# Block products of seven in chunks 1, 3, 4 and 5 of three feed-forward nets, and their sums kept in PSUM

## The chip, the cores and the metric

One core of a Trainium2 chip runs the whole program once. The metric is the device time of one execution in microseconds; the kernel before is given by the median of three runs. The profile is of one further execution of the same program.

## The reference

Two layers; each has a feed-forward net, a mixer, a cross attention and a second feed-forward net, with a layer norm after each. Sequence 256, width 1024, all in f32. Only the nets matter here:

```python
D_MODEL, SEQ, DEPTH, D_FF = 1024, 256, 2, 2816

def swiglu(x, w_gate, w_up, w_down):
    return (jax.nn.silu(x @ w_gate) * (x @ w_up)) @ w_down

for l in range(DEPTH):
    h = layer_norm(ALPHA * h + 0.5 * swiglu(h, ffn1_gate[l], ffn1_up[l], ffn1_down[l]), ...)   # nets 1 and 3
    ...
    h = layer_norm(ALPHA * h + 0.5 * swiglu(h, ffn2_gate[l], ffn2_up[l], ffn2_down[l]), ...)   # nets 2 and 4
```

The nets are called 1 to 4 in the order in which they run. Net 1 has inputs of its own to set up and takes other branches (`early is not None`).

## The kernel before

**Products.** Every f32 operand is split in two: a rounded high part (`split`, L75, a cast on ACT, `whi`) and the rest (L76, a subtraction on DVE, `wlo`). A product is three matmuls, high by high, high by low, low by high (`mm_rows`, L156 to L159, which calls L132). A weight piece is 128x1024 f32, 512 KB; it is loaded into a `raw` tile and split once, one ACT cast and one DVE subtraction for each.

**A net** (`ffn`) works through D_FF in six chunks: five of 512 columns (0 to 4) and one of 256 (5). A chunk multiplies x by its gate and up columns, and `silu(gate) * up` (`sg`) is transposed: `turn` sends `sg` through four DMAs (`dealt`, L525), two DVE transposes (L531), and one split into `ah` (ACT, L75) and `al` (DVE, L76). The product with the down weights (`both`, 24 matmuls into the `dn` banks for one pair of down pieces) needs `ah` and `al`.

A chunk of 512 is computed in one of two ways:

- `hidden` (chunk 0: `first`): 8 weight pieces, 96 matmuls of 512 columns, two DVE products of gate and up (L514).
- `by_seven`: x (2 token tiles by 2 halves of the depth) times (gate, up by the same halves) is a product of 2x2 blocks; the Winograd form needs seven block products in place of eight, 84 matmuls. It has 14 weight pieces to split and 4 sums of weight blocks on DVE (L702). The gate and up blocks are w00, w10, w01, w11. Three more block sums are made by DMAs that add into SBUF (`more`, L738, issued by POOL). Sums and differences of x come from `blocks_of_x` (`quarters`, L653 and L661, split into kTh and kTl).

Chunk 5 by seven is the same at 256 columns (84 matmuls of 256), with three block sums more made by DVE and fewer pieces (7 of 128x1024).

**Which chunk goes which way:** `sevens`, L821. In nets 2 to 4: 2, 4 and 5; in net 1: 2 and 4. The products with the down weights are handed out by `todo`: every by_seven chunk of 512 does two `both`s between its block products (`between[0]` after the third, `between[1]` after the fourth), and `later` says how many come after a chunk of the other kind.

**Sums in by_seven:** a block product is summed in PSUM (`o[0]` runs on through all of them); what is needed of it on the way is copied to SBUF (`taken`, L734, ACT) and added or subtracted there by DVE (`put`, L721, four times a chunk).

**Homes:** w00's two pieces lie in `homes[0]`. For the net's first by_seven chunk these are the tiles `spare0` and `spare1`, which hold `quarters` before.

**The order** of each engine's queue is fixed when the program is built, by a scheduler, and every engine and the DMA queue of SP work strictly in their order. `issue_after` and `manual_schedule` tie single places by hand.

Of the kernel before, what the change touches and what calls it, by code (L numbers as in the profile page):

```python
# [11 lines left out]
AF = mybir.ActivationFunctionType  # L12
ALU = mybir.AluOpType
# [47 lines left out]
def model(ctx: ExitStack, tc: tile.TileContext, t: dict, out: bass.AP):  # L61
    nc = tc.nc
# [11 lines left out]
    def split(hi, lo, src):  # L74
        rounded = nc.scalar.copy(hi, src)  # L75
        lows.append(nc.vector.tensor_tensor(lo, src, hi.bitcast(F32), op=ALU.subtract))  # L76
        return rounded
# [398 lines left out]
    def ffn(l, name, n, pend=None, last=False, early=None, started=None, following=None):  # L476
        gate, up, down = (t[f"{name}_{x}"][l] for x in ("gate", "up", "down"))
        with tc.tile_pool(name="ffn", bufs=2, reuse_waits="tile") as fp:
            acts = []
# [23 lines left out]
            def ordered(v):  # L503
                return v.rearrange("p (a k j) -> p a k j", a=4, j=32)

            def in_order(o):
                return o.rearrange("p (a j k) -> p a k j", a=4, j=32)

            def activate(s, i, og):
                return nc.scalar.activation(ordered(s[:, i, :]), in_order(og), AF.Silu)  # L510
# [154 lines left out]
            def by_seven(c0, ncol, bx, between):  # L665
                deep = 1024 // ncol

                def rows_by_columns(r):
                    return r.rearrange("p (k c) -> p k c", c=ncol)

                def pieces(*tags):
                    return [
                        rows_by_columns(
                            (fp if "spare" in g else wp).tile([P, DM], F32, tag=g, name="raw", bufs=6 if g == "raw" else 1)
                        )
                        for g in tags
                    ]

                def part_of(m, j, i):
                    k = 4 * j + deep * i  # L680
                    return m[k * P : (k + deep) * P, c0 : c0 + ncol].rearrange("(k p) c -> p k c", p=P)

                def block(m, j, to):
                    for i, x in enumerate(to):
                        loads.append(nc.sync.dma_start(x, part_of(m, j, i)))
                    return to

                if ncol == CHUNK:
                    homes = [("spare0", "spare1"), ("lng", "lnb"), ("raw", "raw")]
                    n = sevens.index(c0 // CHUNK)  # L690
                    homes = [homes[(n + i) % 3] for i in range(3)] + [("spare2", "raw")]
                else:
                    homes = [("spare2",), ("raw",), ("raw",), ("raw",)]
                w00 = block(gate, 0, pieces(*homes[0]))
                w01 = block(up, 0, pieces(*homes[1]))
                w10 = block(gate, 1, pieces(*homes[3]))

                def parts_of(r, plus=None):
                    hi, lo = [], []
                    for i in range(len(r)):  # L700
                        if plus is not None:
                            nc.vector.tensor_tensor(r[i], r[i], plus[i], op=ALU.add)  # L702
                        h = wp.tile([P, 1024], F32R, tag="whi", name="whi", bufs=8)
                        w = wp.tile([P, 1024], F32R, tag="wlo", name="wlo", bufs=8)
                        h, w = (rows_by_columns(x) for x in (h, w))
                        split(h, w, r[i])
                        hi.append(h)
                        lo.append(w)
                    return Weights(hi, lo, deep, [])

                def part_of_x(i, j):
                    d = slice(4 * j, 4 * j + 4)
                    return xTh[:, d, tok(i)], xTl[:, d, tok(i)]

                def run(o, x, w, more=False):
                    for k in range(4):
                        wh, wl = w.at(k, slice(0, ncol))
                        mm_rows(o, x[0][:, k, :], x[1][:, k, :], wh, wl, k == 0 and not more, k == 3, more)

                def put(o, a, op, b):  # L720
                    nc.vector.tensor_tensor(ordered(o), in_order(a), ordered(b), op=op)  # L721

                if ncol == CHUNK:
                    s, ef = activations(), fp.tile([P, NT, CHUNK], F32, tag="up", name="halves", bufs=1)
                else:
                    both = fp.tile([P, DM], F32, tag="spare0", name="both", bufs=1)
                    s, ef = both.rearrange("p (a i c) -> a p i c", a=2, i=NT)
                e, f = ef[:, 0, :], ef[:, 1, :]

                def bank():  # L730
                    return acc((P, CHUNK))[:, 0:ncol]

                def taken(o, bank):
                    return nc.scalar.copy(ordered(o), in_order(bank))  # L734

                def more(to, m, j):
                    for i, x in enumerate(to):
                        nc.gpsimd.dma_start(x, part_of(m, j, i), accum_op=ALU.add)  # L738

                o = [bank() for _ in range(3)]  # L740
                run(o[0], part_of_x(0, 0), parts_of(w00))
                taken(s[:, 0, :], o[0])
                run(o[1], bx[0], parts_of(w00, w01))
                more(w01, up, 1)
                run(o[2], part_of_x(0, 1), parts_of(w10))
                between[0]()
                put(s[:, 0, :], o[2], ALU.add, s[:, 0, :])
                w11 = block(up, 1, pieces(*homes[2]))
                run(o[0], bx[1], parts_of(w00, w11), True)
                if ncol == CHUNK:  # L750
                    more(w00, gate, 1)
                copied = taken(e, o[0])
                between[1]()
                nc.scalar.activation(s[:, 0, :], s[:, 0, :], AF.Silu)
                put(e, o[1], ALU.subtract, e)
                if ncol == CHUNK:
                    run(o[0], bx[2], parts_of(w01), True)
                    taken(f, o[0])
                    o.append(bank())
                    run(o[3], bx[3], parts_of(w11))  # L760
                    put(f, o[1], ALU.subtract, f)
                    run(o[0], part_of_x(1, 1), parts_of(w00), True)
                else:
                    o.append(bank())
                    run(o[3], bx[3], parts_of(w11))
                    run(o[0], bx[2], parts_of(w01), True)
                    taken(f, o[0])
                    put(f, o[1], ALU.subtract, f)
                    with tc.issue_after(copied.ins):
                        w = parts_of(w00, w10)  # L770
                    between[2]()
                    run(o[0], part_of_x(1, 1), w, True)

                def left():
                    act = activate(s, 1, o[0])
                    put(e, o[3], ALU.add, e)

                    def gate_all():
                        passed.append((act, nc.vector.tensor_tensor(s, s, ef, op=ALU.mult)))
                        return turn(s)  # L780

                    return gate_all

                return left
# [33 lines left out]
                return w, ah[:, 2 * u : 2 * u + 2, :], al[:, 2 * u : 2 * u + 2, :]  # L818


            sevens = (2, 4) if early is not None else (2, 4, 5)  # L821
            passed, dealts, turn_memory = [], [], None
            bx = []

# [20 lines left out]
                            rows_of(a, i, k, m, c == u == k == 0, apart)  # L845

            todo = [(c, u) for c in range(4) for u in range(2)]
            later = (0, 0, 0, 2, 0, 2) if early is None else (0, 1, 0, 1, 0, 2)
            for c, (c0, ncol) in enumerate(chunks):
                if not c:  # L850
                    acts.append(first()())
# [11 lines left out]
                    )  # L863
                else:
                    acts.append(hidden(c0)() if ncol == CHUNK else last_hidden(c0, turn_memory))
                if c == 1 and early is None:
                    bx.extend(blocks_of_x())
                if c == 5:
                    gb = ln_params(l, n)
# [9 lines left out]
                if c in sevens:  # L879
                    if ncol < CHUNK:  # L880
                        held = []
                        with tc.issue_after(lows[-1].ins):
                            acts[4] = acts[4](held)
                    acts.append(left() if c + 1 in sevens else left()() if c == 5 else left()()())
                    if ncol < CHUNK:
                        with tc.issue_after(passed[-1][0].ins), tc.issue_after(passed[-1][1].ins):
                            held[0]()
                        both(3, 1)
                else:
                    for _ in range(later[c]):  # L890
                        both(*todo.pop(0))
# [569 lines left out]
```

## Time and profile before

| | |
|---|---|
| runs, median (lowest to highest) | 1062.99 us (1062.97 to 1064.28) |
| the profiled execution, span | 1061.1 us |
| PE busy | 99%, 6014 matmul records |
| DVE busy | 88% |
| ACT busy | 62% |
| mean granted TensorE clock | 0.998 |
| net 1, about | 8 to 175 us |
| net 2, about | 364 to 530 us |
| net 3, about | 531 to 697 us |
| net 4, about | 887 to 1061 us |

A matmul's record lasts 0.38 us, but one starts every 0.216 us: matmuls are pipelined, and a busy share of PE overstates it. Where the chain of waits runs on PE, its rows give the time of a run of matmuls directly. DVE's operations overlap a little in the same way; what counts is the time from one start to the next. In a timeline row stand the start, the time, engine, line, operation, out<-in, and the count of rows merged.

### The profile page before, as it was taken

The page shows a single profiled execution, that of the slowest core. Times are in us where ns is not written, and L with a number is a line of the kernel's source. Part 1 is how long each engine was busy: PE and PEld are TensorE (multiplying, and loading weights), DVE is VectorE, ACT ScalarE, POOL GpSimd, SP SyncE. Part 2 cuts the span into 40 slices and gives each one's busy share as a digit, 9 for nine tenths or more (in the row PEclk, how much of TensorE's full clock was granted, in tenths as well). Part 3 has the DMA queues.
Part 4 walks back from the last instruction along what each step waited for, and adds up shares of the span by engine and source line. Part 5 has one row for each costly group of instructions (what it writes and reads, how often), then busy time and mean ns, then how long its engine had stood idle before and what let it go on. Part 6 is the DMA issues. An engine that isn't in the chain of part 4 may idle for free.

```text
span 1061.1 us, 16496 instructions
## 1 busy us (share of the span) xinstructions
PE 1051.2 (99%) x6014; PEld 934.8 (88%) x6014; DVE 933.2 (88%) x1246; ACT 662.0 (62%) x909; POOL 94.7 (9%) x128
## 2 busy tenths in 40 slices
PE   9999999999999999999999999999999999999996
PEld 7888888889899888889888888998998998888896
DVE  6998898989988789887898987999899787898787
ACT  6675775676557566655665656666774655675661
POOL 8002001000000001010001001010000000000001
PEclk9999999999999999999999999999999999999999
DMA  9999984854675589988789978866636675799971
GB/s 364 296 320 280 260 272 146 268 166 155 210 271 179 171 281 231 363 192 217 239 305 254 338 224 208 271 233 222 206 122 215 241 243 162 242 303 294 241 194 68
DMA packets 142306, 251.06 MB, mean 237 GB/s; under 512 B 11249, under 2 KB 51985, under 8 KB 142225
## 3 DMA queue, kind: packets, MB, share of 16 engines
q1 hardware_dynamic: 130656, 228.89, 65.0%
q0 software_dynamic: 10992, 19.94, 10.9%
q10 hardware_dynamic: 576, 1.18, 0.3%
q8 instruction: 47, 0.77, 0.3%
q14 instruction: 35, 0.28, 0.1%
HBM read 234.50 MB, written 1.05 MB: 222 GB/s over the span
## 4 chain that ended last, share of the span: by engine, by line
PE 92%; DVE 3%; DMA 2%; issue 2%; ACT 1%; POOL 0%; DVEq 0%; ACTq 0%; POOLq 0%
PE acc L132 61%; PE dn L132 27%; DVE wlo L76 2%; PE acc L199 1%; DMA raw<-in_ffn_gate_dram 1%; DMA raw<-in_ffn_down_dram 1%; ACT whi L75 0%; PE dn L1139 0%; DVE raw L702 0%; PE dn L1213 0%; DMA lng<-in_ln_g_dram 0%; DMA h<-in_x_dram 0%; DVE al L76 0%; PE acc L581 0%; DVE square L531 0%
## 5 line engine op out<-in xcount | busy, mean ns | idle before, releaser
L75 ACT CAST whi<-raw 128x1024 fp32r<-128x1024 f32 (+1 forms) x452 | 456.1, 1042 | 201.2 <-PE dn L132 58.0
L76 DVE TENSOR_TENSOR wlo<-raw,whi 128x1024 fp32r<-128x1024 f32 (+1 forms) x452 | 534.5, 1211 | 53.1 <-ACT whi L75 47.1
L132 PE MATMUL acc<-whi,xT 128*128 128x512 f32 (+1 forms) x1064 | 313.9, 372 | 0.0
L132 PEld LDWEIGHTS acc<-whi,xT 128*128 128x128 f32 x1064 | 199.0, 189 | 26.9 <-DVE xT L76 0.3
L132 PE MATMUL acc<-wlo,xT 128*128 128x512 f32 (+1 forms) x532 | 197.9, 372 | 0.0
L132 PE MATMUL dn<-whi,ah 128*128 128x512 f32 x346 | 131.5, 380 | 0.0
L132 PE MATMUL dn<-wlo,ah 128*128 128x512 f32 x346 | 131.3, 379 | 0.0
L132 PE MATMUL dn<-whi,al 128*128 128x512 f32 x346 | 131.1, 379 | 0.0
L132 PE MATMUL acc<-xT,whi 128*128 128x512 f32 x480 | 117.6, 381 | 0.0
L132 PEld LDWEIGHTS acc<-wlo,xT 128*128 128x128 f32 x532 | 100.6, 189 | 13.4
L132 PEld LDWEIGHTS acc<-xT,whi 128*128 128x128 f32 x480 | 86.8, 190 | 9.8
L132 PE MATMUL dn<-whi,xT 128*128 128x512 f32 x288 | 87.7, 380 | 0.0
L132 PEld LDWEIGHTS dn<-wlo,ah 128*128 128x128 f32 x346 | 65.4, 189 | 9.6 <-DVE wlo L76 0.6
L132 PEld LDWEIGHTS dn<-whi,al 128*128 128x128 f32 x346 | 65.4, 189 | 9.2
L132 PEld LDWEIGHTS dn<-whi,ah 128*128 128x128 f32 x346 | 65.4, 189 | 9.0
L132 PEld LDWEIGHTS acc<-xT,wlo 128*128 128x128 f32 x480 | 62.9, 191 | 3.2
L132 PE MATMUL acc<-xT,wlo 128*128 128x256 f32 x480 | 63.2, 275 | 0.0
L132 PE MATMUL acc<-wlo,kTh 128*128 128x512 f32 (+1 forms) x176 | 61.7, 351 | 0.0
L132 PE MATMUL acc<-whi,kTl 128*128 128x512 f32 (+1 forms) x176 | 61.7, 351 | 0.0
L132 PE MATMUL acc<-whi,kTh 128*128 128x512 f32 (+1 forms) x176 | 61.7, 351 | 0.0
L132 PEld LDWEIGHTS dn<-whi,xT 128*128 128x128 f32 x288 | 54.4, 189 | 7.6
L132 PE MATMUL dn<-wlo,xT 128*128 128x512 f32 x144 | 54.6, 379 | 0.0
(252 smaller groups left out, 1296.8 us busy)
## 6 DMA issues: line engine op xcount, KB each, us to landing
raw<-in_ffn_up_dram SPq DMA_DIRECT2D x88, 512.0 KB, 5.7
raw<-in_ffn_down_dram SPq DMA_DIRECT2D x88, 512.0 KB, 5.6
raw<-in_ffn_gate_dram SPq DMA_DIRECT2D x84, 512.0 KB, 5.6
raw<-in_w_in_dram SPq DMA_DIRECT2D x48, 512.0 KB, 4.8
dealt<-sg SPq DMA_DIRECT2D x80, 128.0 KB, 4.5
raw<-in_ffn_up_dram POOLq DMA_DIRECT2D x19, 512.0 KB, 6.3
raw<-in_ffn_gate_dram POOLq DMA_DIRECT2D x16, 512.0 KB, 9.4
raw<-in_ca_k_dram SPq DMA_DIRECT2D x16, 512.0 KB, 5.2
```

The source lines that it names most:

```text
L75: rounded = nc.scalar.copy(hi, src)
L76: lows.append(nc.vector.tensor_tensor(lo, src, hi.bitcast(F32), op=ALU.subtract))
L132: turns.append(nc.tensor.matmul(o, w, x, start=start, stop=stop, skip_group_check=more))
L199: turns.append(nc.tensor.transpose(pt[:, k, :], src[:, (4 * j + k) * P : (4 * j + k + 1) * P], unit))
```

## The change

In nets 2 to 4 the chunks by seven become 1, 3, 4 and 5; chunk 2 goes the other way. `blocks_of_x` is called after chunk 0 in place of chunk 1. No `both` is left outside of by_seven chunks. Net 1 keeps its chunks.

In every by_seven chunk, net 1's too, the sums move into PSUM: after the first block product ACT copies the bank `o` to a second bank `total`, on which later products accumulate while `o` goes on to the gate of the first token tile; after the fourth product, ACT writes minus `total` into a bank `less`, which the product with w11 accumulates on. DVE's four `put`s become two.

```diff
-                o = [bank() for _ in range(3)]
-                run(o[0], part_of_x(0, 0), parts_of(w00))
-                taken(s[:, 0, :], o[0])
-                run(o[1], bx[0], parts_of(w00, w01))
+                o, total, one = (bank() for _ in range(3))
+                run(o, part_of_x(0, 0), parts_of(w00))
+                nc.scalar.copy(total, o)
+                run(one, bx[0], parts_of(w00, w01))
+                taken(e, one)
                 more(w01, up, 1)
-                run(o[2], part_of_x(0, 1), parts_of(w10))
+                run(o, part_of_x(0, 1), parts_of(w10), True)
                 between[0]()
-                put(s[:, 0, :], o[2], ALU.add, s[:, 0, :])
+                activate(s, 0, o)
                 w11 = block(up, 1, pieces(*homes[2]))
-                run(o[0], bx[1], parts_of(w00, w11), True)
+                run(total, bx[1], parts_of(w00, w11), True)
                 if ncol == CHUNK:
                     more(w00, gate, 1)
-                copied = taken(e, o[0])
+                less = bank()
+                copied = nc.scalar.mul(less, total, -1.0)
                 between[1]()
-                nc.scalar.activation(s[:, 0, :], s[:, 0, :], AF.Silu)
-                put(e, o[1], ALU.subtract, e)
                 if ncol == CHUNK:
-                    run(o[0], bx[2], parts_of(w01), True)
-                    taken(f, o[0])
-                    o.append(bank())
-                    run(o[3], bx[3], parts_of(w11))
-                    put(f, o[1], ALU.subtract, f)
-                    run(o[0], part_of_x(1, 1), parts_of(w00), True)
+                    run(total, bx[2], parts_of(w01), True)
+                    put(f, e, ALU.subtract, total)
+                    run(less, bx[3], parts_of(w11), True)
+                    run(total, part_of_x(1, 1), parts_of(w00), True)
...
                 def left():
-                    act = activate(s, 1, o[0])
-                    put(e, o[3], ALU.add, e)
+                    act = activate(s, 1, total)
+                    put(e, e, ALU.add, less)
...
-            sevens = (2, 4) if early is not None else (2, 4, 5)
+            sevens = (2, 4) if early is not None else (1, 3, 4, 5)
...
-            later = (0, 0, 0, 2, 0, 2) if early is None else (0, 1, 0, 1, 0, 2)
+            later = (0, 0, 0, 0, 0, 0) if early is None else (0, 1, 0, 1, 0, 2)
...
-                if c == 1 and early is None:
+                if c == 0 and early is None:
                     bx.extend(blocks_of_x())
...
-                    acts.append(left() if c + 1 in sevens else left()() if c == 5 else left()()())
+                    acts.append(left() if c == 4 and 5 in sevens else left()() if c == 5 else left()()())
```

Over the whole program PE has 36 matmuls of 512 columns less (4149 to 4113), DVE 18 splits (L76) and 12 sums of weight blocks (L702) more, 16 `put`s and 6 gate products (L514) less and three long products `sg` times `halves` more, ACT 18 casts more, POOL 12 adding DMAs more; SP's count of DMAs is the same.

What this does to the queues is shown for net 3 at three places. First DVE, from the last of the quarters on. Before, the quarters and their low parts (kTl) stand between the pieces of chunk 1 (`raw_5555` and the like are pieces of hidden chunk 1; `acc_5500` is the up product of chunk 0):

```order
L661 TENSOR_TENSOR quarters_5380<-quarters_5379,quarters_5380 128x512
L76 TENSOR_TENSOR wlo_5548<-raw_5543,whi_5547 128x1024
L76 TENSOR_TENSOR wlo_5552<-raw_5544,whi_5551 128x1024
L76 TENSOR_TENSOR kTl_93<-quarters_5379,kTh_92 128x512
L76 TENSOR_TENSOR wlo_5560<-raw_5555,whi_5559 128x1024
L76 TENSOR_TENSOR kTl_93<-quarters_5380,kTh_92 128x512
L76 TENSOR_TENSOR wlo_5564<-raw_5556,whi_5563 128x1024
L76 TENSOR_TENSOR wlo_5624<-raw_5619,whi_5623 128x1024
L76 TENSOR_TENSOR wlo_5628<-raw_5620,whi_5627 128x1024
L514 TENSOR_TENSOR sg_5381<-acc_5500,sg_5381 128x512
```

Now the quarters come in one piece, and behind them the first split of w00 (`raw_5571`, `raw_5572`, in spare0 and spare1; 5575 and 5576 are w01, 5691 and 5692 are w11). The L514 of chunk 0's second tile stands behind the first two splits:

```order
L661 TENSOR_TENSOR quarters_5395<-quarters_5394,quarters_5395 128x512
L76 TENSOR_TENSOR kTl_93<-quarters_5394,kTh_92 128x512
L661 TENSOR_TENSOR quarters_5395<-quarters_5395 128x512
L76 TENSOR_TENSOR kTl_93<-quarters_5395,kTh_92 128x512 x2
L76 TENSOR_TENSOR wlo_5589<-raw_5571,whi_5588 128x1024
L702 TENSOR_TENSOR raw_5571<-raw_5571,raw_5575 128x1024
L76 TENSOR_TENSOR wlo_5593<-raw_5572,whi_5592 128x1024
L514 TENSOR_TENSOR sg_5396<-acc_5515,sg_5396 128x512
L76 TENSOR_TENSOR wlo_5611<-raw_5571,whi_5610 128x1024
L702 TENSOR_TENSOR raw_5572<-raw_5572,raw_5576 128x1024
```

DVE's queue goes on from there without a gap, with w10 (5579, 5580) and the first pair of down pieces (5654, 5655) up to the low part `al` of chunk 0:

```order
L702 TENSOR_TENSOR raw_5571<-raw_5571,raw_5691 128x1024
L76 TENSOR_TENSOR wlo_5616<-raw_5572,whi_5615 128x1024
L76 TENSOR_TENSOR wlo_5635<-raw_5579,whi_5634 128x1024
L76 TENSOR_TENSOR wlo_5639<-raw_5580,whi_5638 128x1024
L76 TENSOR_TENSOR wlo_5659<-raw_5654,whi_5658 128x1024
L76 TENSOR_TENSOR wlo_5663<-raw_5655,whi_5662 128x1024
L531 STREAM_TRANSPOSE square_5548<-dealt_5541 128x4x4x32 x2
L76 TENSOR_TENSOR wlo_5697<-raw_5571,whi_5696 128x1024
L702 TENSOR_TENSOR raw_5572<-raw_5572,raw_5692 128x1024
L76 TENSOR_TENSOR al_5547<-square_5548,ah_5546 128x1024
```

So `al` of chunk 0 now stands behind 13 operations on whole pieces that begin with w00. The third place is PE, where chunk 1 has done its first three block products (`acc_5585` is `o`, `acc_5586` is `total`) and comes to the first `both`:

```order
L132 MATMUL acc_5585<-whi_5638,xT_89 128x512
L132 MATMUL acc_5586<-whi_5696,kTh_92 128x512
L132 MATMUL dn_5553<-whi_5658,ah_5546 128x512
L132 MATMUL dn_5553<-wlo_5659,ah_5546 128x512
L132 MATMUL dn_5554<-whi_5658,ah_5546 128x512
L132 MATMUL dn_5554<-wlo_5659,ah_5546 128x512
L132 MATMUL dn_5555<-whi_5658,ah_5546 128x512
L132 MATMUL dn_5555<-wlo_5659,ah_5546 128x512
L132 MATMUL dn_5556<-whi_5658,ah_5546 128x512
L132 MATMUL dn_5556<-wlo_5659,ah_5546 128x512
```

After these come three more of `total` and then the first matmul that reads `al_5547`. Before, the first `both` (in chunk 2) came a whole chunk of 96 matmuls later, in plain order. In nets 2 and 4 the same rows stand at the same places.

More of the change, by code (lines that the diff above doesn't have):

```diff
@@ L720, in put @@
                 def put(o, a, op, b):
-                    nc.vector.tensor_tensor(ordered(o), in_order(a), ordered(b), op=op)
+                    nc.vector.tensor_tensor(ordered(o), ordered(a), in_order(b), op=op)
                 if ncol == CHUNK:
@@ L753, in by_seven @@
+                copied = nc.scalar.mul(less, total, -1.0)
                 between[1]()
-                nc.scalar.activation(s[:, 0, :], s[:, 0, :], AF.Silu)
-                put(e, o[1], ALU.subtract, e)
                 if ncol == CHUNK:
-                    run(o[0], bx[2], parts_of(w01), True)
-                    taken(f, o[0])
-                    o.append(bank())
-                    run(o[3], bx[3], parts_of(w11))
-                    put(f, o[1], ALU.subtract, f)
-                    run(o[0], part_of_x(1, 1), parts_of(w00), True)
-                else:
[L764 to L768, printed above, removed]
+                    run(total, bx[2], parts_of(w01), True)
+                    put(f, e, ALU.subtract, total)
+                    run(less, bx[3], parts_of(w11), True)
+                    run(total, part_of_x(1, 1), parts_of(w00), True)
+                else:
+                    run(less, bx[3], parts_of(w11), True)
+                    run(total, bx[2], parts_of(w01), True)
+                    put(f, e, ALU.subtract, total)
@@ L771, in by_seven @@
                     between[2]()
-                    run(o[0], part_of_x(1, 1), w, True)
+                    run(total, part_of_x(1, 1), w, True)
                 def left():
-                    act = activate(s, 1, o[0])
-                    put(e, o[3], ALU.add, e)
+                    act = activate(s, 1, total)
+                    put(e, e, ALU.add, less)
                     def gate_all():
```

## The prediction

> **What bounds the kernel now.** I read the page's busy table first, and then asked the chain of waits, net by net, whether PE's 99% is real. The chain over net 3 answers it: its pieces have a start, a time and a count of matmuls.
>
> ```profile
> PE 1051.2 (99%) x6014; PEld 934.8 (88%) x6014; DVE 933.2 (88%) x1246; ACT 662.0 (62%) x909; POOL 94.7 (9%) x128
> ```
>
> ```profile
> 531.04 7.77 PE acc L132 x36
> 538.81 0.87 PE acc L199 x8
> 539.68 41.44 PE acc L132 x192
> 581.12 5.18 PE dn L132 x24
> ...
> 653.64 11.79 PE acc L132 x72
> 665.43 2.59 PE dn L132 x12
> ...
> 694.11 0.87 PE acc L338 x8
> ```
>
> Each piece begins where the one before it ends, from 531.0 to 694.1, with no other engine between. 41.44 us for 192 matmuls are 0.216 us each, 36 of 256 columns among the x72 take 4.02, 0.112 each. So net 3 is bound by PE without a gap, and a matmul taken out is worth 0.216 us as long as nothing else comes late; equally, a wait that is put in is lost for good. Nets 2 and 4 begin with the same pieces (below). The question is how much room the others have:
>
> ```profile
> 528.00:697.00 169.00, 169.00 (x836) 149.34 (x834) 153.12 (x170) 106.03 (x126) 15.11 (x14) 1.00 0.86 260
> ```
>
> The columns are the stretch, its length, busy time of PE, PEld, DVE, ACT and POOL, the granted clock, the DMA share and GB/s. Over net 3 DVE is busy 153 of 169 us, and the DMA engines 86%. There are 16 us of slack on DVE in a net, and it works in strict order, so slack late in the net does not help early in it.
>
> **What is taken out.** A chunk of 512 by seven has 84 matmuls in place of 96. Net 2 to 4 each get one such chunk more, so 36 matmuls go, as the counts of the two programs confirm: 36 x 0.216 = **-7.8 us**.
>
> **What DVE gets.** Fourteen splits for eight and four sums are 10 operations on whole pieces more; two gate products go and two `put`s and one long product come; the other chunks by seven lose six `put`s. The rows for the price of each:
>
> ```profile
> 635.07 6.90 DVE L76 TENSOR_TENSOR wlo<-raw,whi 128x1024 fp32r<-128x1024 f32 x6
> 641.88 0.69 DVE L721 TENSOR_TENSOR sg<-acc,sg 128x512 f32<-128x512 f32 x1
> ...
> 674.40 1.29 DVE L531 STREAM_TRANSPOSE square<-dealt 128x512 f32<-128x512 f32 x2
> 675.62 1.18 DVE L76 TENSOR_TENSOR wlo<-raw,whi 128x1024 fp32r<-128x1024 f32 x1
> ```
>
> Six splits take 6.81 us from start to start, 1.136 each; two transposes take 1.22. Operations of 512 columns are 0.60 apart (the timeline below). A net's DVE work grows by 10 x 1.136 for the splits and sums, 1.14 for the long product, less about 3 for `put`s: some 9.5 us. It fits into 16 us less the 2.6 that PE saves, but barely; chunks 2 to 5 of the new order hold 70 whole-piece operations, 8 of 512 and 6 transposes, 88 us, beside 97.6 us of PE. That is cover enough if nothing comes late.
>
> **Where it does not fit: the start of chunk 1.** This is the term that decides. Net 3's quarters on DVE before:
>
> ```profile
> 541.79 1.29 DVE L653 TENSOR_TENSOR quarters<-xT 128x512 f32<-128x512 f32 x2
> 543.00 0.69 DVE L661 TENSOR_TENSOR quarters<-quarters 128x512 f32<-128x512 f32 x1
> 543.60 0.69 DVE L514 TENSOR_TENSOR sg<-acc,sg 128x512 f32<-128x512 f32 x1
> 544.20 0.69 DVE L661 TENSOR_TENSOR quarters<-quarters 128x512 f32<-128x512 f32 x1
> ```
>
> Now eleven such operations follow each other from 541.8, 0.604 apart, to 548.4. The eighth is the last to read spare0, at 546.7; the eleventh the last of spare1, at 548.5. Only then may SP issue w00's two pieces into these tiles. The same load stood there before:
>
> ```profile
> 548.99 1.50 SPq L685 DMA_DIRECT2D raw<-in_ffn_gate_dram  x2
> ```
> ```profile
> raw<-in_ffn_gate_dram SPq DMA_DIRECT2D x1, 512.0 KB, 5.3
> ```
> ```profile
> L75 ACT CAST whi<-raw 128x1024 fp32r<-128x1024 f32 x444 | 451.1, 1050 | 201.0 <-PE dn L132 58.0 <-PE acc L132 44.0 <-DVE raw L702 36.9
> L75 ACT CAST ah<-square 128x1024 fp32r<-128x1024 f32 x20 | 20.9, 1045 | 3.2 <-DVE square L531 3.2
> ```
>
> The first of the pair landed 5.3 us after its issue (it went into spare0; nothing needed it for 8 us). So the first piece lands at 552.0, its cast ends at 553.05, and DVE, which stood idle from 548.4, begins the queue shown in the section on the change: 13 whole pieces (14.8), one L514 (0.6), two transposes (1.2), and `al` itself (1.2): 17.8 us, to **570.9**. The second piece lands at 553.8 and is cast by 554.9, in time for the third of these. ACT keeps up, since a cast takes 1.05 to DVE's 1.14.
>
> PE ends chunk 0 at 539.68 + 60 x 0.216 = 552.6. Its queue holds 36 matmuls of three block products, 8 of the down product that need only `ah`, and 3 of `total` before the first that reads `al`: 47, which would end at 562.8. It gets there at 570.9: a stall of **8.1 us**. Behind the waiting matmul stand all the rest of PE's queue, and behind PE the ACT casts that wait for buffers.
>
> Nets 2 and 4:
>
> ```profile
> 372.79 41.44 PE acc L132 x192
> ```
> ```profile
> 375.80 0.69 DVE L661 TENSOR_TENSOR quarters<-quarters 128x512 f32<-128x512 f32 x1 [0.65 <-ACT quarters L202]
> ```
> ```profile
> 895.96 41.44 PE acc L132 x192
> ```
> ```profile
> 899.06 0.69 DVE L661 TENSOR_TENSOR quarters<-quarters 128x512 f32<-128x512 f32 x1 [0.65 <-ACT quarters L202]
> ```
>
> Net 2's chunk 0 ends at 372.79 + 12.95 = 385.74. From 375.8, six operations to spare0's last reader: 379.5; landed 384.8, cast 385.85, `al` 403.65, where 385.74 + 10.15 = 395.9 was wanted: 7.8. Net 4 has the same rows 523.2 later: 7.8. Together **+23.7 us**.
>
> **Bounds of that term.** From below: if the piece were there when DVE has ended the quarters, the queue alone gives 548.4 + 17.8 - 562.8 = 3.4 in net 3, 381.3 + 17.8 - 395.9 = 3.2 in the others, 9.8 in all. From above: w00 lands as late as the adding DMAs do, 9.4 us (the page's part 6, POOL), 4.1 more in each net: 36. I take the 5.3 of the same load in the same tile.
>
> **Smaller terms.** The seeds: ACT writes `total` and `less` into PSUM, which no row shows; the nearest are its copies out of PSUM.
>
> ```profile
> L734 ACT COPY halves<-acc 128x512 f32<-128x512 f32 x16 | 9.3, 584 | 1.6 <-PE acc L132 1.6
> L152 ACT COPY sums<-acc 128x256 f32<-128x256 f32 x32 | 12.0, 374 | 12.8 <-PE acc L132 9.0 <-DVE qTl L76 2.3 <-DVE kTl L76 1.5
> ```
>
> In chunks of 512 a `both` of 5.2 us hides the second seed, two block products the first. In chunk 5 only three matmuls (0.65) lie between the product before `less` and the one on it, beside 0.37 for the copy and two handovers: I take 0, with 0 to 1 us a net. For waits in chunks 3 to 5, where 88 of 97.6 us on DVE are taken, I take 0.6 a net, **+1.8**, with 0 to 5. The added DMA work (2 MB a net through POOL's queue) I cost at nothing beyond this: the stall leaves room for it; without that cover it is the second rival. Net 1 gets the seeds but no chunk more, and lies as dense: 0, with -1 to 1.
>
> **Sum.** -7.8 + 23.7 + 1.8 = **+17.7 us**. The profiled execution's span is 1061.1, and 1.9 lie around it to the median of 1063.0; so 1078.8 for the span, and **1081** for the median.
>
> **Rivals.**
>
> *The stall does not come, and it is faster.* It would need `al` within 2.6 us of the wanted time, so w00 split-ready by 562.8 + 2.6 - 17.8 = 547.6 in net 3; DVE is busy with the quarters until 548.4, and the load may only start at 546.7. For it speaks only that pieces of the rows could be shorter in the new surroundings. It gives 1063 - 7.8 = 1055. 5%.
>
> *DVE's queue alone.* w00 lands unexpectedly early: 9.8 in place of 23.7, so 1063 - 7.8 + 9.8 + 1 = 1066. 8%, and 5% more for something between it and no change.
>
> *Chunks 3, 4 and 5 stall too.* Three in a row with block sums by POOL. For it:
>
> ```profile
> 573.38:601.90 28.52, 28.52 (x134) 24.95 (x133) 27.01 (x28) 20.50 (x23) 2.37 (x2) 1.00 1.07 329
> ```
> ```profile
> raw<-in_ffn_gate_dram POOLq DMA_DIRECT2D x16, 512.0 KB, 9.4
> ```
>
> While one such chunk ran, the DMA share was 1.07, and an adding DMA takes 9.4 us to land, about what DVE's rows between its issue and its use last (10 us). If each comes 4 us late once a net in addition, it is 12 more: 1093. Against it: PE's stall in chunk 1 gives DVE and DMA a lead of several us. 16%.
>
> *The clock falls in the stall.* PE's longest single gap would be about 3 us, from the end of the third product (565.0) to `ah` (568.4).
>
> ```profile
> 1053.00:1057.00 4.00, 0.11 (x1) 0.00 (x0) 3.75 (x9) 0.00 (x0) 0.92 (x1) 1.00 0.00 0
> 1057.00:1061.00 4.00, 0.00 (x0) 0.00 (x0) 0.29 (x1) 0.00 (x0) 0.00 (x0) 0.58 0.37 133
> ```
>
> After the last matmul the granted clock is still 1.00 through 4 us without work, and 0.58 in the next 4. A gap of 3 should pass; if not, 4 us at half speed cost 2 in each net: 1087. 6%. The Trainium skill, "TensorE: Matmul & The Clock Gate", section "Why this matters for your kernels", asks for no PE gap above about 3 us, and says that an idle window puts the clock back to half; by that rule our gap is on the edge. The two rows agree that the clock falls with idleness, later than the rule has it.
>
> *The change does not do what it says* is excluded by the counts above.
>
> **Chances.** The forecast, 1075 to 1087, 60%; the rivals as given (5, 13, 16, 6). 1066 to 1096 leaves out the faster case, a few per cent about no change, and the far end of the third rival. Faster by over 0.2% (2.1 us, about what a measurement of this kernel can tell from no change): 5%; within it: 5%; slower: 90%.
>
> **What would show it.** In the profile after: the chain of nets 2 to 4 leaves PE at the start of chunk 1 and goes back through `al` L76, a run of DVE splits and sums, an ACT cast and the DMA of the gate to the quarters; DVE idle some 4.6 us before the first split of w00; the first `both` starting about 8 us late; from there PE dense again; L132 36 records fewer. I am wrong if DVE's whole pieces before `al` pass at another pace than 1.136, if w00 is issued before the quarters end, or if the later chunks break PE's chain.

## The result, and the profile after

| | before | after |
|---|---|---|
| median (lowest to highest) | 1063.63 us (1062.97 to 1064.44, 4 runs) | 1088.00 us (1085.98 to 1089.07, 4 runs) |
| ratio after to before, 95% interval | | 1.0225 [1.0213, 1.0238] |
| the profiled execution, time and span | span 1061.1 us | 1085.98, span 1084.3 us |
| mean granted TensorE clock, profiled execution | 0.998 | 0.997 |

The kernel became slower by 24.4 us in the medians and 23.2 us in the spans; 17.7 were forecast. The four runs after spread over 3.1 us. The busy row of the page after shows the 36 matmul records less, and 27 us more on DVE:

```profile
PE 1054.0 (97%) x5978; PEld 927.2 (86%) x5978; DVE 960.0 (89%) x1257; ACT 684.1 (63%) x936; POOL 109.2 (10%) x140
```

The chain of waits, which stood on PE alone through nets 2 to 4, now leaves PE at the start of chunk 1. In net 3 (start, us, what):

```profile
554.60 4.55 DMA raw<-in_ffn_gate_dram
559.17 1.05 ACT whi L75
560.25 0.98 DVE wlo L76
561.99 1.22 DVE wlo L76
563.21 2.27 DVE raw L702 x2
...
571.14 1.31 DVE square L531 x2
572.47 1.05 ACT ah L75
573.57 1.99 PE dn L132 x8
...
586.57 31.08 PE acc L132 x144
```

This is the load of w00 into the quarters' tiles, its cast, the run of splits and sums on DVE, the transposes, and the first `both`; behind it PE is dense for a whole chunk. DVE's timeline of the same place has the idle time and its end (in brackets: idle before, and what ended it):

```profile
553.10 1.47 DVE L76 TENSOR_TENSOR kTl<-quarters,kTh 128x512 fp32r<-128x512 f32 x2
557.46 1.23 DVE L76 TENSOR_TENSOR wlo<-raw,whi 128x1024 fp32r<-128x1024 f32 x1 [2.89 <-ACT whi L75]
...
560.25 1.23 DVE L76 TENSOR_TENSOR wlo<-raw,whi 128x1024 fp32r<-128x1024 f32 x1 [0.30 <-ACT whi L75]
...
574.59 1.22 DVE L76 TENSOR_TENSOR al<-square,ah 128x1024 fp32r<-128x1024 f32 x1
```

**How the time adds up.** For each matmul in PE's timeline I took the time to the next start, less 0.216 us (0.112 for 256 columns), and summed what is left over. Before, under 0.5 us is left in any of these nets.

| us not covered by matmuls | net 2 | net 3 | net 4 | sum |
|---|---|---|---|---|
| up to the end of chunk 1 | 6.5 | 7.5 | 8.8 | 22.8 |
| chunks 3 to 5 | 1.9 | 2.9 | 3.4 | 8.2 |

31.0 less the 7.8 of the 36 matmuls is 23.2, the difference of the spans. Some matmul records are missing in the trace, so an entry can be off by some tenths of a us. A wait is written smaller than what it costs: the longest one below as 2.84, but from start to start 3.22 pass where 0.22 were due, so 3.0 are lost. Such a loss is called a hole here. Of net 3's 7.5 up to the end of chunk 1 the longest hole is 3.0; the rest lies ahead of it, most of it in three holes of 1.0, 1.0 and 0.7 us, where the first three block products wait for the casts and splits of their pieces.

**Net 4's extra.** All three nets have the same 3.0 us hole ahead of the first matmul on `ah`. PE's timeline after it, net 3 first, then net 4:

```profile
570.35 0.38 PE L132 MATMUL acc<-whi,kTh 128*128 128x512 f32 x1
573.57 0.48 PE L132 MATMUL dn<-whi,ah 128*128 128x512 f32 x1 [2.84 <-ACT ah L75]
573.89 0.38 PE L132 MATMUL dn<-wlo,ah 128*128 128x512 f32 x1
574.10 0.38 PE L132 MATMUL dn<-whi,ah 128*128 128x512 f32 x1
...
934.77 0.38 PE L132 MATMUL acc<-whi,kTh 128*128 128x512 f32 x1
937.99 0.80 PE L132 MATMUL dn<-whi,ah 128*128 128x512 f32 x1 [2.84 <-ACT ah L75]
...
939.43 0.63 PE L132 MATMUL dn<-wlo,ah 128*128 128x512 f32 x1
939.85 0.63 PE L132 MATMUL dn<-whi,ah 128*128 128x512 f32 x1
```

In net 3 the matmuls go on 0.21 to 0.22 apart, in net 4 0.42 to 0.43: eight of them take 3.47 us (937.99 to 941.46) where net 3 needs 1.83. The granted clock in windows of 3.41 us (last three columns: clock, DMA share, GB/s) says why; net 3 first, then net 4:

```profile
569.29:572.70 3.41, 1.44 (x7) 0.93 (x5) 3.41 (x5) 1.69 (x3) 0.00 (x0) 1.00 1.06 360
572.70:576.11 3.41, 2.54 (x12) 2.24 (x13) 3.38 (x4) 2.16 (x3) 1.19 (x1) 1.00 0.96 317
934.52:937.93 3.41, 0.63 (x3) 0.20 (x2) 3.41 (x5) 1.70 (x3) 0.00 (x0) 1.00 1.03 383
937.93:941.35 3.42, 3.36 (x8) 2.74 (x9) 3.39 (x4) 2.17 (x4) 1.18 (x1) 0.50 0.90 273
```

The borders are those of the trace's own record of the clock: in every kept trace it changes only at points that lie a whole multiple of 3.41 us apart. A hole of 3.0 us may fall inside one such stretch or across two. In net 4 it fell inside: the matmuls make up 0.14 of the stretch before 937.93 (0.216 us for each), and the next stretch ran at half clock. In net 3 they make up 0.37, in net 2, where the hole lies across a border, 0.58 and 0.51, and the clock stayed. The last section gives the same count for all traces.

### The profile page after: what moved, and what is told of

The parts are those of the page before. It is cut to its first block, busy times and chain, and to the rows that moved or that the text cites. A ratio compares the mean times of both kernels' runs of the same rounds, so it can differ in the third digit from the quotient of the medians.

```text
span 1084.3 us, 16502 instructions
## 1 busy us (share of the span) xinstructions
PE 1054.0 (97%) x5978; PEld 927.2 (86%) x5978; DVE 960.0 (89%) x1257; ACT 684.1 (63%) x936; POOL 109.2 (10%) x140
## 4 chain that ended last, share of the span: by engine, by line
PE 72%; DVE 12%; DMA 8%; issue 5%; ACT 3%; SPq 0%; DVEq 0%; ACTq 0%
PE acc L132 46%; PE dn L132 24%; DVE wlo L76 5%; DMA raw<-in_ffn_gate_dram 5%; ACT whi L75 2%; DMA raw<-in_ffn_up_dram 2%; DVE raw L702 1%; DMA dealt<-sg 1%; DVE h L412 1%; DVE quarters L661 1%; PE acc L199 1%; PE dn L1135 0%; DVE kTl L76 0%; DVE h L407 0%; DVE xT L76 0%
## 5 line engine op out<-in xcount | busy, mean ns | idle before, releaser
L76 DVE TENSOR_TENSOR wlo<-raw,whi 128x1024 fp32r<-128x1024 f32 (+1 forms) x470 | 553.5, 1208 | 61.8 <-ACT whi L75 56.8
L75 ACT CAST whi<-raw 128x1024 fp32r<-128x1024 f32 (+1 forms) x470 | 472.1, 1041 | 199.5 <-DVE raw L702 56.0
L132 PE MATMUL acc<-whi,xT 128*128 128x512 f32 (+1 forms) x944 | 280.1, 373 | 4.5 <-ACT whi L75 3.2
L132 PEld LDWEIGHTS acc<-whi,xT 128*128 128x128 f32 x944 | 176.4, 189 | 31.5 <-ACT whi L75 6.0
L132 PE MATMUL acc<-wlo,xT 128*128 128x512 f32 (+1 forms) x472 | 175.8, 373 | 2.2 <-DVE wlo L76 2.2
L132 PEld LDWEIGHTS acc<-wlo,xT 128*128 128x128 f32 x472 | 89.3, 189 | 15.8 <-DVE wlo L76 4.4
L132 PE MATMUL acc<-whi,kTh 128*128 128x512 f32 (+1 forms) x224 | 80.5, 359 | 2.6 <-ACT whi L75 2.6
L132 PE MATMUL acc<-wlo,kTh 128*128 128x512 f32 (+1 forms) x224 | 80.8, 361 | 1.8 <-DVE wlo L76 1.8
L132 PE MATMUL acc<-whi,kTl 128*128 128x512 f32 (+1 forms) x224 | 79.9, 357 | 0.0
L702 DVE TENSOR_TENSOR raw<-raw 128x1024 f32<-128x1024 f32 x53 | 64.2, 1218 | 0.5
```

The source lines that it names most:

```text
L132: turns.append(nc.tensor.matmul(o, w, x, start=start, stop=stop, skip_group_check=more))
```

## The experiments

Three theories. **A**: the loss is the start of chunk 1, a load held back by the quarters and a queue on DVE ahead of `al`. **B**: the seeds in PSUM cost it. **C**: four chunks by seven a net are too much for DVE and the DMA queues, wherever they stand. Each run is compared with the kernel before, timed on the same chip; its median there lay between 1063.4 and 1064.0 us.

### The seeds without the new chunks

```diff
-            sevens = (2, 4) if early is not None else (1, 3, 4, 5)
+            sevens = (2, 4) if early is not None else (2, 4, 5)
```

`later`, the place of `blocks_of_x` and the condition on `left` are as before, too.

> Chunks by seven 2, 4 and 5 as before, only the sums moved into seeded PSUM banks. Theory A (the loss is the first `both` of chunk 1, which waits for `al` behind a load held back by the quarters and a queue on DVE): no stall in chunk 1 or 2, 1063 to 1066, 0 to 1 us a net in chunk 5. Rival B (the seeds cost: the extra ACT copies and the handover between banks hold PE up): the waits now seen in chunk 3 and chunk 5 of the changed kernel, some 0.6 + 0.6 + 0.5 us a net, stand here too: 1068 to 1069; if the seeds also made the stall in chunk 1, over 1075.

Measured: 1064.16 us, ratio 1.0004 [0.9995, 1.0013]. PE waits once in nets 2 to 4, in net 4's chunk 2, and not in chunk 5, where up to 1 us was expected (the table of waits):

```profile
PE acc L132 <- DVE halves L721: 1.6, 1, 1.6
```

So B falls: the seeds cost nothing that can be measured (1.4 us at the upper end of the interval), and the waits in chunks 3 and 5 of the changed kernel aren't theirs. The kernel before has no such wait of 1.6 us; whether it comes from the seeds was not tried.

### The new chunks without the seeds

The chunks, `later`, `blocks_of_x` and `left` of the change, with the sums of the kernel before (SBUF, four `put`s).

> Chunks by seven 1, 3, 4 and 5, but the sums as before, in SBUF with four DVE `put`s. Theory A: the same stall at the first `both` of chunk 1, so 1084 to 1091 (up to 2 us a net of DVE work more, less what the seeds cost in chunk 5). Rival B: without the seeds the gain of 7.8 us shows, 1056 to 1065.

Measured: 1086.62 us, 1.0221 [1.0207, 1.0235]. With the run above, the whole loss, within the spread of the runs, belongs to the choice of chunks.

### Chunk 1 alone

```diff
-            sevens = (2, 4) if early is not None else (1, 3, 4, 5)
+            sevens = (2, 4) if early is not None else (1, 4, 5)
-            later = (0, 0, 0, 0, 0, 0) if early is None else (0, 1, 0, 1, 0, 2)
+            later = (0, 0, 0, 2, 0, 0) if early is None else (0, 1, 0, 1, 0, 2)
```

> The changed kernel with chunks by seven 1, 4 and 5, three a net as before, so no matmul less than before; the two `both`s of chunk 1 are done after the hidden chunk 3. Theory A: the stall in chunk 1 comes whole (22.7 us measured in the changed kernel, 1.7 of it the lower clock in net 4), the later waits (8.5 us) mostly go: 1064 + 21 to 24 = 1084 to 1089. Rival C (four a net are what costs): 1063 to 1068.

Measured: 1086.74 us, 1.0214 [1.0196, 1.0231]: 22.6 us above the seeds on (2, 4, 5), with as many matmuls; only the first chunk by seven stands one earlier. The chain of net 3 has the same hole, and behind it PE without a break:

```profile
573.92 1.99 PE dn L132 x8
...
586.92 49.21 PE acc L132 x228
636.13 10.36 PE dn L132 x48
```

In net 4 the hole is 4.1 us, with 6.8 us at half clock behind it. The waits in chunks 3 to 5 are gone. So A holds for the 22.8 us, and the 8.2 us behind it belong to three chunks by seven in a row (a part of C).

### w00 in another home

```diff
-                    homes = [homes[(n + i) % 3] for i in range(3)] + [("spare2", "raw")]
+                    homes = [homes[(n + i + (early is None)) % 3] for i in range(3)] + [("spare2", "raw")]
```

The edit turns the homes of all three blocks, in every chunk by seven of 512 columns in nets 2 to 4: in chunk 1, w11 now goes into the quarters' tiles.

> The changed kernel with the homes rotated by one in nets 2 to 4: w00 of chunk 1 goes to lng and lnb, not to the tiles that hold the quarters, so its load can start before the quarters end. Theory A: the idle time of DVE between the quarters and the first split of w00 (2.9 + 0.3 us in net 3) goes and the queue of 13 whole pieces stays: chunk 1's 22.7 us fall to about 10, 1073 to 1080; al of net 3 some 3.2 us earlier. Rival B or C (four chunks by seven are too much for DVE and the DMA queues wherever they stand): unchanged or later waits take it back, 1085 to 1089.

Measured: 1080.83 us, 1.0157 [1.0141, 1.0172], just outside what was expected. DVE is busy without a gap from the quarters on, so the idle time went; the first split of w00 now stands ahead of the last two low parts of the quarters, the second right behind them. But PE waits all the same, now at the fourth block product, and the clock falls (PE's timeline, net 3):

```profile
565.00 0.38 PE L132 MATMUL acc<-whi,xT 128*128 128x512 f32 x1
567.81 0.56 PE L132 MATMUL acc<-whi,kTh 128*128 128x512 f32 x1 [2.43 <-ACT whi L75]
569.07 0.80 PE L132 MATMUL acc<-wlo,kTh 128*128 128x512 f32 x1 [0.70 <-DVE wlo L76]
569.66 0.63 PE L132 MATMUL acc<-whi,kTl 128*128 128x512 f32 x1
```

Up to the end of chunk 1 the three nets now lose 5.1, 6.6 and 5.4 us, 17.1 in place of 22.8. Of this, 10.4 are holes, near the 10 that were expected, and the rest is matmuls at half pace, which stand partly in place of waiting, since DVE sets the pace here. The clock fell once in each net, for 3.4, 6.8 and 3.4 us; in net 3 at 568.08, one matmul behind the hole of 2.6 us and before the second hole was over.

### The first `both` later

```diff
-                        [lambda: both(*todo.pop(0))] * 2 if ncol == CHUNK else
+                        ([lambda: None, lambda: [both(*todo.pop(0)) for _ in range(2)]] if c == 1 else [lambda: both(*todo.pop(0))] * 2) if ncol == CHUNK else
```

> The changed kernel, only the first `both` of chunk 1 is handed out after the fourth block product, beside the second. If `al` alone is late (theory A in its narrow form), PE reaches it 12 matmuls, 2.6 us, later, and each stall shrinks by 2.6: 1088 - 7.8 = 1080. If DVE's whole queue is late (the sums and splits of w00 and w11 stand ahead of `al` in it), the fourth product waits in its place and little is won: 1084 to 1088.

Measured: 1080.78 us, 1.0162 [1.0147, 1.0177]. The number is that of the narrow theory, but by luck: the timeline shows the other one (net 3):

```profile
571.51 0.48 PE L132 MATMUL acc<-whi,kTh 128*128 128x512 f32 x1 [0.55 <-ACT whi L75]
572.77 0.48 PE L132 MATMUL acc<-wlo,kTh 128*128 128x512 f32 x1 [0.78 <-DVE wlo L76]
...
573.95 0.38 PE L132 MATMUL dn<-whi,ah 128*128 128x512 f32 x1
```

`ah` and `al` are in time, and the fourth product waits 1.75 us (start to start) in place of the 3.0 on `ah`. So 1.3 of the 2.6 us is won in each net. The rest goes with the clock: no hole is longer than 1.1 us any more, the trace has no half clock before the end of the program, the four runs have 0.998 or 0.999 and 1080.54 to 1080.87 us, where the changed kernel has 0.994 to 0.997 and 1085.98 to 1089.07. Between the profiled executions lie 5.2 us (1084.3 and 1079.1): about 3.9 of holes and the 1.6 at half clock.

### Both of these together

> The changed kernel with w00 of chunk 1 in lng and lnb and with the first `both` of chunk 1 behind the fourth block product: each of the two alone gave 1080.8. If they take away two separate causes, their gains of 7.2 add up: 1073 to 1075. If both only uncover DVE's queue of sums and splits ahead of the fourth block product, little comes on top: 1077 to 1081.

Measured: 1082.92 us (1079.61 to 1085.12), 1.0168 [1.0152, 1.0184], above both ranges. Nothing adds up. In net 3 a third wait has taken over, the turn of chunk 0 itself (chain):

```profile
560.99 0.61 DVE sg L514
...
563.70 6.59 DMA dealt<-sg
...
572.77 1.05 ACT ah L75
573.87 12.31 PE dn L132 x48
```

`sg`'s product (L514) stands behind w00's first pieces on DVE, its four DMAs take 6.6 us to land (4.8 in the median), and `ah` is as late as ever. In the changed kernel this wait stood close behind: there the last of the four landed at 568.85, 2.3 us before DVE came to the transposes at 571.14. The profiled execution is the slowest of the four; the clock fell in each net, after holes of 3.2, 2.9 and 4.0 us.

### The sums of weight blocks on POOL

```diff
-                            nc.vector.tensor_tensor(r[i], r[i], plus[i], op=ALU.add)
+                            (nc.vector if early is not None else nc.gpsimd).tensor_tensor(r[i], r[i], plus[i], op=ALU.add)
```

> The changed kernel with the sums of weight blocks (L702) of nets 2 to 4 on POOL in place of DVE; no row shows what such a sum takes there. If DVE's queue ahead of `al` is the larger part of the stall, two to four whole pieces of 1.136 us go from it: 2.3 to 4.5 us a net, 1075 to 1081. If POOL takes over 2 us for a sum, or its adding DMAs come later behind the sums, the chain through it takes that back: 1086 or more.

The same with chunks 2, 3, 4 and 5:

> Chunks by seven 2, 3, 4 and 5 (1074.7 with the sums on DVE) and the sums of weight blocks on POOL. The wait left there is 3 to 4.6 us a net in chunk 4, on the adding DMA of the gate, issued when DVE has split w00 + w11. If DVE's load decides when that is issued, it goes with 4.5 us less of DVE work a chunk: 1060 to 1066. If the DMA engines (share 1.0 from 570 to 660 us) decide, 1072 to 1077; slower if POOL's sums delay its own DMAs.

Measured: 1155.22 us, 1.086 [1.0844, 1.0877], and 1144.56 us, 1.0769 [1.075, 1.0789]. The groups of the first:

```profile
L76 DVE TENSOR_TENSOR wlo<-raw,whi 128x1024 fp32r<-128x1024 f32 (+1 forms) x470 | 626.3, 1367 | 105.9 <-ACT whi L75 100.4 <-PE acc L132 3.8 <-DMA raw<-in_ca_k_dram 0.2
...
L702 POOL TENSOR_TENSOR raw<-raw 128x1024 f32<-128x1024 f32 x45 | 133.7, 2975 | 239.1 <-DVE wlo L76 222.9 <-DMA raw<-in_ffn_up_dram 16.2
```

A sum takes 2.975 us on POOL (1.218 on DVE in the changed kernel), and DVE's splits grow from a mean of 1208 ns there to 1367. DVE is relieved of 45 sums and still busier (981.2 us for 960.0). The Trainium skill, "SBUF — State Buffer", section "Who interferes with whom", says that a DVE instruction with two SBUF inputs, as a split is, contends with a GpSimd instruction that reads SBUF; the slower splits agree with it. So these two runs say nothing on DVE's load by itself.

### Chunks 2, 3, 4 and 5

```diff
-            sevens = (2, 4) if early is not None else (1, 3, 4, 5)
+            sevens = (2, 4) if early is not None else (2, 3, 4, 5)
```

> The changed kernel with chunks by seven 2, 3, 4 and 5: the same number of matmuls, but the first chunk by seven no longer follows the quarters and chunk 0's `al` at once. Theory A: the 22.7 us of chunk 1 go; three in a row then ask DVE for about 29.7 us a chunk beside 28.5 on PE, 1 to 3 us a net: 1063 to 1073. Rival C: the load of four stays and only its place changes, 1080 to 1090.

Measured: 1074.73 us, 1.0098 [1.0084, 1.0112]. The start is clean, as A has it; PE loses 0.6 us in chunk 3, and then 2.9, 3.9 and 4.7 us (nets 2, 3 and 4) in one place, ahead of the last product of chunk 4. The chain there in net 3:

```profile
647.30 10.73 DMA raw<-in_ffn_gate_dram
658.05 1.05 ACT whi L75
659.13 0.07 DVE wlo L76
...
660.27 1.23 DVE wlo L76
661.52 1.22 DVE raw L702
662.75 0.61 DVE halves L721
...
663.49 4.56 PE acc L132 x14
```

The gate's adding DMA lands too late; while the three chunks run, the DMA share is 0.98 to 1.01. If it is late by what was lost bit by bit over three such chunks, less work on PE ahead of it early and more late should help; the next run tries that.

### The same, with the products with the down weights dealt out anew

One `both` in chunk 2, two in chunk 3, three in chunk 4:

```diff
-                        [lambda: both(*todo.pop(0))] * 2 if ncol == CHUNK else
+                        [lambda: both(*todo.pop(0)), lambda: [both(*todo.pop(0)) for _ in range(c - 2 if early is None else 1)]] if ncol == CHUNK else
```

> Chunks by seven 2, 3, 4 and 5 (1074.7) with one `both` in chunk 2, two in chunk 3 and three in chunk 4, in place of two in each: the last block product of chunk 4, which waited 3 to 4.6 us in each net for the adding DMA of the gate, comes 5.2 us later behind the others, that of chunk 2 5.2 us earlier. If the wait is a lag that builds up over three chunks, it goes, and the lower clock behind it: 1062 to 1067. If chunk 2 has no 5 us to spare, its last product waits in its place: 1070 to 1078.

Measured: 1064.12 us, 1.0004 [0.9996, 1.0013]. What PE still waits for in net 3 (us in total, times, longest); with two in each chunk it was 3.7 us on `halves` alone:

```profile
PE acc L132 <- ACT whi L75: 1.0, 1, 1.0
PE dn L132 <- ACT whi L75: 0.4, 1, 0.4
PE dn L132 <- DVE wlo L76: 0.3, 1, 0.3
PE acc L132 <- DVE wlo L76: 0.2, 1, 0.2
```

The lag was one that builds up: 10.6 us come back by giving PE other work ahead of the late product, among them two stretches at half clock that the trace of the run before has and this one has not. Whether DVE or the DMA engines lack the time in such chunks is not shown: the chain goes through both, and the runs with the sums on POOL could not part them. Dealt out in halves, one and a half, two, two and a half (the code is left out here):

> As the run with one, two and three `both`s in chunks 2, 3 and 4 (1064.1), but one and a half, two, and two and a half: the last block product of chunk 2, still 0.7 to 1.2 us late there, comes 2.6 us later and should not wait, that of chunk 4 comes 2.6 us earlier and would be 0.4 to 2 us late. If the lags are as sized, what is won in chunk 2 is about given back in chunk 4: 1062 to 1065, no clear difference from before; under 1061 it would beat both kernels.

Measured: 1063.25 us, 0.9996 [0.9987, 1.0005]. What is left of holes (1.2, 2.8 and 2.7 us in the three nets) takes nearly all of the 7.8 us of the 36 matmuls back; no version that was run beat the kernel before.

## Why the prediction was right, and by how much it was off

**The direction, and 36 matmuls: right.** The balance of the spans closes with 7.8 us. The median of 1088.0 lies within 1066 to 1096, but 1 us above the 1075 to 1087 that had 60%. One of the signs of being wrong did come: the later chunks broke PE's chain, which the forecast had dense again behind the stall.

**The stall at the first `both` of chunk 1: right in place and mechanism.** Net 3 comes 5.9 us later than before, by net 2's own loss (the first matmul behind the transposes of x starts at 545.34, 539.44 before), so the forecast's times are read with 5.9 added. w00's load should be issued at 546.7 + 5.9 = 552.6; SP's timeline has:

```profile
552.61 2.35 SPq L685 DMA_DIRECT2D raw<-in_ffn_gate_dram  x2
```

and ACT's, for the cast that waits for its first piece:

```profile
556.39 1.04 ACT L75 CAST whi<-raw 128x1024 fp32r<-128x1024 f32 x1 [2.05 <-DMA raw<-in_ffn_gate_dram]
```

`al` was to be ready at 570.9 + 5.9 = 576.8 and was at 575.7 (574.59 and 1.14). DVE's idle time was 2.9 + 0.3 us where 4.6 were expected: the two pieces landed in about 3.8 and 4.55 us, not in 5.3. So the stalls were 6.5, 7.5 and, without the lower clock, some 7.2 us, 21.2 together, where 23.7 were forecast. The pace of DVE, 1.136 us a piece, held (five splits in 5.69 us, from 565.45 to the transposes at 571.14).

**Which wait ends last: half right.** The forecast named `al`. In the trace `ah` ended the longest wait, at 573.57, as the forecast had it only in its rival on the clock, and `al`, ready at 575.73, was 0.3 us ahead of its own turn, at 576.05. The two lie so close that the time came out much the same. The runs with another home and a later `both` show why the name matters little: the fourth block product and the turn of chunk 0 stand close behind, and each of them takes the place of the wait that is removed.

**The clock: named, and thought too unlikely.** It was given 6% and 2 us in each net. In the profiled run it fell in one net of three, which cost 1.6 us. The forecast let a gap of 3 us pass because 4 us without work at the end of the program had passed at full clock; what counts in the traces is not the length of a gap but how little work one stretch of 3.41 us holds. The other runs of the changed kernel have 0.995, 0.994 and 0.994 where the profiled one has 0.997, and 1.0 to 3.1 us more; a fall costs 0.0016 of the mean clock (half of 3.41 us in 1084). So one or two more falls fit the median's 2 us above the profiled run; those runs left no trace that would show them.

**The seeds: right at 0.** ACT's copy and negation take 0.57 and 0.58 us as the nearest rows had them (0.58), and the run with the seeds alone shows no cost beyond the noise.

**The step that was mis-sized: the waits in chunks 3 to 5.** The forecast put 0.6 us a net there, 1.8 in all, with 5 as the far end, since the stall would give DVE and the DMAs a lead. It measured 8.2. It counted 88 us of DVE's work against 97.6 of PE's over chunks 2 to 5 together. Chunks 1, 4 and 5 show none of these waits, chunks 3, 4 and 5 and chunks 2, 3 and 4 do: the sum over four chunks hid a lack that holds only while such chunks follow each other. The lead that the stall was to give did not last. This was the rival in which chunks 3, 4 and 5 stall too, at two thirds of the 12 us that it was given. Too large a stall, -2.5, a lower clock, +1.6, and too small a later wait, +6.4, make the 5.5 us between the forecast and the measured span.

## What to carry to other kernels

A load into a tile that is being read starts only when the last reader ends (here at 552.61, behind a reader that ended at 552.59); so look at what the first piece of a moved stage lands in, and what stands in the strict queue between it and the operand that the bottleneck wants. Slack counts per stage, not per net: three stages in a row that each need a little more than they have fall behind by a sum that shows in one place. There, giving the bottleneck other work ahead of the late operand brought back 10.6 us. At chunk 1, removing a named cause brought back 7.2 us, and the next wait stood behind it. No run put the turn of chunk 0 ahead of w00's pieces on DVE, so what that order alone costs is not shown.

## What the runs showed of the hardware

- Three holes of 3.0 us on PE, of the same length in the same program: after two of them the matmuls went on at 0.216 us, after one at 0.43 us for 3.5 us. The Trainium skill, "TensorE: Matmul & The Clock Gate", section "HAM oscillation — how this bites in real kernels", names idle gaps over about 3.4 us as the ones that bring the clock back to half; here a hole of 3.0 did, and one of 3.0 did not, and with w00 in its other home one of 2.6 did. In the section "What's actually happening" it says that the watch is on a free-running window; that agrees, since the changes of the clock lie on a grid of 3.41 us wherever the holes are.
- The thirteen kept traces tell what such a stretch of 3.41 us needs. I counted what share of it the matmuls fill, each by its pace at full clock (0.216 us for 512 columns, 0.112 for 256, others by their columns). All 42 stretches at full clock with a share of up to 0.36 were followed by half clock, and none of the 3986 with over 0.39; of the 11 between, two were. Of the stretches at half clock, the 15 with up to 0.37 were followed by another, the 31 with 0.40 and more by full clock. Net 3's hole, at 0.37, just passed.
- The four runs of the kernel with the later `both`, whose trace has no fall, lie within 0.3 us; those of the other kernels with holes of 2.6 us and more spread over 2.5 to 5.5 us. The spread alone proves nothing: the kernel before, without holes, spreads over 1.7 to 2.6 us in its 7 to 15 runs.
- The same load of 512 KB into the same tile landed in 3.8 us here, and in 5.3 before.
- A sum of two blocks of 128x1024 in f32 took 2.975 us on POOL beside a busy DVE, 2.4 times as long as on DVE.
